# A two-layer decoder trunk: the second layer's attention by heads instead of by groups, its numerators weighted row by row

## The chip, the cores and the metric

The kernel runs on one core of one Trainium2 chip. The metric is the time of an execution on the device, in microseconds (us); lower is better. Before the change three runs took 2020.91, 2022.48 and 2024.51 us. Five engines work side by side, each through a list of instructions of its own: TensorE (PE, matrix products), VectorE (DVE), ScalarE (ACT), GpSimd (POOL) and SyncE (SP, which issues the transfers).

## What is computed

The reference runs two layers over a stream of 1024 positions of 1024 features, in fp32. Layer A is an mLSTM mixer; the change touches it in one place only. Layer B is attention in three dilation groups with eight heads of 128, each followed by a residual and a layer norm. Cut to what matters:

```python
def dilated_block_attention(qb, kb, vb, dilation, n_back, slopes):
    ...
    m = sc.max(-1)
    e = jnp.exp(sc - m[..., None])
    den = e.sum(-1)
    o = jnp.einsum('nbhqk,nbkhd->nbqhd', e, vb.astype(jnp.float32)) / jnp.moveaxis(den, 2, 3)[..., None]
    lse = jnp.moveaxis(m + jnp.log(den), 2, 3)
    return o, lse

def dilated_attention_layer(x, w_in, w_out, kv_blocks, slopes):
    proj = x @ w_in
    q_all = proj[..., :N_GROUPS_B * INNER_B].reshape(bsz, s, N_GROUPS_B, HEADS_B, HEAD_DIM_B)
    z = proj[..., N_GROUPS_B * INNER_B:]
    for g, (window, dilation) in enumerate(GROUPS_B):
        ...
    wts = jax.nn.softmax(jnp.stack(lses), axis=0)
    o = jnp.sum(wts[..., None] * jnp.stack(outs), axis=0).reshape(bsz, s, INNER_B)
    y = o.astype(x.dtype) * jax.nn.silu(z)
    return y @ w_out
```

For every head there are three groups, and in each a softmax over 256 (group 0 and 1) or 128 keys (group 2). The groups' outputs are then mixed by a softmax over their log-sum-exp, row by row; this is the same as dividing the sum of the weighted numerators by the sum of the weighted denominators.

## The kernel before

**Products.** Every large product is made in three passes of reduced precision: an operand is split into a high part (a cast on ScalarE, L93) and a low part (a subtract on VectorE, L94), and `mm3` (L96 to L100) issues high x high, high x low and low x high. On top stands Strassen's scheme with seven products instead of eight: `strassen_steps` (L188) for products of 512 columns, a generator that gives way after each of its seven products (12 matmuls each), and `strassen_wide` (L291) for those of 1024, with 48 matmuls per product, whose weight sums (L313, by `sums`) and result sums (L317) run on VectorE.

**Order.** The program is written once, and a scheduler of the framework then sets the order of each engine's list by a model of its own; `issue_after(x)` keeps what is inside behind instruction x. A tile's slot or a PSUM bank that is given twice makes the second user wait for the first. So the order of the text, the slots and these marks set the order of the work.

**Layer B.** It begins at about 985 us. Two quads of four heads each are the outer loop; inside it come the three groups, and inside a group the four heads. `values(g, quad)` makes the group's values with `strassen_wide` in the first quad, and loads them from memory in the second. Then per head:

- `queries_keys` (a `strassen_steps` of 84 matmuls of 512 columns), with L1201 and L1210 evacuating;
- `scores`: matmuls of 128 columns, row maxima with the bias added (L1260, VectorE), and exponentials with the row sum (L1264, ScalarE) into `stat`;
- `attend`: the blocks of exponentials are transposed on PE (L1278), split, and multiplied by the values (mm3 and the whole matmuls L1301 and L1332); the group's output is copied from PSUM into slot 13 (L1340) and stored to memory as `og`, 512 KB.

After a head's third group, `factors` (L1345) transposes `stat` (L1347), stores it (L1351) and loads it back with eight small transfers. `merge` makes the three groups' factors on 8 partitions and stores them as `f` (L1394). `fetch` loads the three outputs and, spread over 128 partitions, the three rows of factors (512 KB each), and `combine` (L1415 to L1419) multiplies and adds them on VectorE in whole tiles of 128 x 1024, with the gate z last. `by_group` does so for the fourth head. The result, `y2`, is stored.

The gates z are four `strassen_steps` of two heads each. Three of them lie among the groups (`gate_at`); the last, for heads 6 and 7, comes behind all heads, and head 7's attend is interleaved with it. Then follows the output projection: for eight blocks of rows, eight blocks of features `c` and two halves `dm`, `block` issues three matmuls, with operands split by `self.split` in 128 x 1024. Its results are taken up by the layer norm (`begin`, `finish`).

## Time and profile before

| | |
|---|---|
| median of the three runs | 2022.48 us |
| the profiled execution | 2017.29 us |
| its span | 2015.5 us |
| granted clock of PE, mean | 0.996 |
| bytes moved | 300.65 MB |
| layer A, layer B, output projection begin at about | 0, 985, 1915 us |

The profile is of one execution. A row of the timeline has the start, the duration, the engine, the line, the operation and, in brackets, how long the engine had nothing to do before it and what released it. Matmuls overlap, so the duration of one (0.39 us at 512 columns) is longer than the distance to the next. Lines are those of the kernel before, where nothing else is said.

### The profile page before, as it was taken

How to read it: one execution, taken by the hardware profiler on the slowest of the kernel's cores; microseconds unless marked ns; L12 is line 12 of the kernel's file. 1: busy time of each engine (PE TensorE's matmuls, PEld its weight loads, DVE VectorE, ACT ScalarE, POOL GpSimd, SP SyncE). 2: the span in 40 equal slices, each digit the busy share in tenths (PEclk: the TensorE clock that was granted, in tenths of full speed). 3: DMA queues.
4: the chain of work that ended last, by engine and by line, in shares of the span. 5: the costliest groups of instructions: out<-in, count | busy, mean ns of one | idle time of the engine just before them, and what ended most of it. 6: DMA issues, size and time to landing. Idle time of an engine off the chain costs nothing.

```text
span 2015.5 us, 26595 instructions
## 1 busy us (share of the span) xinstructions
PE 1962.4 (97%) x9521; PEld 1626.3 (81%) x9521; DVE 1444.8 (72%) x2854; ACT 992.5 (49%) x1990; POOL 158.7 (8%) x127
## 2 busy tenths in 40 slices
PE   9999999999999999999999999999999999999997
PEld 7778888778888888878788888877887788887776
DVE  8778778675577776457867765776568887776878
ACT  5455555535645543343524542565255456676621
POOL 0200000022145343000000000000000000000000
PEclk9999999999999999999999999999999999999999
DMA  4445464456754543526121143225325622224753
GB/s 170 146 164 193 164 224 172 147 172 227 271 204 164 192 163 117 184 62 232 53 73 53 55 154 106 71 97 178 134 91 203 225 95 85 84 95 154 269 198 126
DMA packets 117916, 300.65 MB, mean 149 GB/s; under 512 B 13652, under 2 KB 31508, under 8 KB 117784
## 3 DMA queue, kind: packets, MB, share of 16 engines
q1 hardware_dynamic: 117784, 298.95, 43.2%
q8 instruction: 75, 1.23, 0.3%
q14 instruction: 57, 0.47, 0.1%
HBM read 206.32 MB, written 92.59 MB: 148 GB/s over the span
## 4 chain that ended last, share of the span: by engine, by line
PE 73%; DVE 12%; DMA 8%; ACT 4%; issue 2%; SPq 0%; POOL 0%; DVEq 0%; ACTq 0%
PE b L98 23%; PE b L100 22%; PE b L99 22%; DVE s L94 3%; DMA s<-in_w_qk 2%; PE b L603 1%; DMA s<-df 1%; ACT s L93 1%; PE b L1278 1%; DMA s<-in_w_z 1%; ACT s L1264 1%; DMA s<-in_xq 1%; PE b L609 1%; PE b L878 1%; DVE s L1415 1%
## 5 line engine op out<-in xcount | busy, mean ns | idle before, releaser
L99 PE MATMUL b<-s,s 128*128 128x512 f32 (+3 forms) x2720 | 1035.3, 382 | 9.2 <-DVE s L94 9.2
L100 PE MATMUL b<-s,s 128*128 128x512 f32 (+3 forms) x2720 | 1021.3, 382 | 4.8 <-DVE s L94 4.7
L98 PE MATMUL b<-s,s 128*128 128x512 f32 (+2 forms) x2720 | 1001.2, 386 | 20.1 <-ACT s L93 16.3
L94 DVE TENSOR_TENSOR s<-s,s 128x512 fp32r<-128x512 f32 (+2 forms) x704 | 507.5, 736 | 279.1 <-ACT s L93 273.4
L93 ACT CAST s<-s 128x512 fp32r<-128x512 f32 (+2 forms) x708 | 436.6, 636 | 541.2 <-PE b L100 308.8
L98 PEld LDWEIGHTS b<-s,s 128*128 128x128 f32 x2720 | 511.7, 188 | 124.7 <-ACT s L93 24.4
L99 PEld LDWEIGHTS b<-s,s 128*128 128x128 f32 x2720 | 512.4, 188 | 107.3 <-DVE s L94 13.2
L100 PEld LDWEIGHTS b<-s,s 128*128 128x128 f32 x2720 | 510.5, 188 | 105.5 <-DVE s L94 9.5
L233 DVE TENSOR_TENSOR s<-s,b 128x512 f32<-128x512 f32 x132 | 89.8, 681 | 27.3 <-PE b L100 25.9
L1264 ACT ACTIVATE s<-s,nmax 128x128 f32<-128x128 f32 (+1 forms) x192 | 84.3, 441 | 45.9 <-DVE nmax L1262 45.6
L94 DVE TENSOR_TENSOR s<-b,s 128x512 fp32r<-128x512 f32 (+1 forms) x96 | 51.5, 552 | 34.7 <-ACT s L93 34.3
L568 DVE SCALAR_TENSOR_TENSOR s<-s,c_convw,s 128x512 f32<-128x512 f32 (+3 forms) x96 | 71.5, 755 | 3.1 <-ACT s L565 2.6
L227 DVE TENSOR_TENSOR s<-s,b 128x512 f32<-128x512 f32 x88 | 59.5, 679 | 16.2 <-PE b L100 11.5
L317 DVE TENSOR_TENSOR s<-s,b 128x512 f32<-128x512 f32 x100 | 63.3, 680 | 8.1 <-PE b L100 7.8
L246 DVE TENSOR_TENSOR s<-s,s 128x512 f32<-128x512 f32 x44 | 30.3, 690 | 50.5 <-DMA s<-in_w_qk 23.5
L812 ACT ACTIVATE s<-s,k 128x128 f32<-128x128 f32 x144 | 47.2, 392 | 39.0 <-DVE s L94 18.5
L313 DVE TENSOR_TENSOR s<-s,s 128x1024 f32<-128x1024 f32 x40 | 49.6, 1247 | 20.8 <-DMA s<-in_w_o 11.7
L1260 DVE CUSTOM_DVE_ANT_0 s<-b,k 128x128 f32<-128x128 f32 (+1 forms) x192 | 57.2, 345 | 6.5 <-PE b L100 4.4
L93 ACT CAST s<-b 128x512 fp32r<-128x512 f32 (+1 forms) x96 | 43.8, 479 | 23.4 <-PE b L100 13.4
L771 POOL TENSOR_TENSOR s<-s 128x512 fp32r<-128x512 f32 x32 | 43.5, 1372 | 75.2 <-ACT s L770 65.5
L1211 DVE SCALAR_TENSOR_TENSOR s<-s,s 128x512 fp32r<-128x512 f32 x48 | 42.4, 885 | 9.6 <-ACT s L1210 9.1
L882 POOL TENSOR_TENSOR s<-s,s 128x512 f32<-128x512 f32 x32 | 42.3, 1337 | 65.0 <-DVE s L881 48.5
(182 smaller groups left out, 1489.0 us busy)
## 6 DMA issues: line engine op xcount, KB each, us to landing
s<-in_w_qk SPq DMA_DIRECT2D x48, 512.0 KB
s<-in_w_out SPq DMA_DIRECT2D x40, 512.0 KB
dp<-s SPq DMA_DIRECT2D x32, 512.0 KB
s<-dp SPq DMA_DIRECT2D x32, 512.0 KB
s<-in_w_v SPq DMA_DIRECT2D x24, 512.0 KB
dg<-s SPq DMA_DIRECT2D x24, 512.0 KB
s<-dg SPq DMA_DIRECT2D x24, 512.0 KB
s<-df SPq DMA_DIRECT2D x24, 512.0 KB
```

What stands on the lines that cost most here:

```text
L93: self.nc.scalar.copy(h, src)
L94: self.last_split = (l_eng or self.nc.vector).tensor_tensor(l, src, f(h), op=ALU.subtract)
L98: mm(ps, lh, rh, start=start, stop=False, skip_group_check=skip)
L99: mm(ps, lh, rl, start=False, stop=False, skip_group_check=skip)
L100: mm(ps, ll, rh, start=False, stop=stop, skip_group_check=skip)
L227: V.tensor_tensor(o, p, q, op=add)
L233: V.tensor_tensor(o, p[lane][rows], q[lane][rows], op=add)
L313: eng.tensor_tensor(o[j], p[j], q[j], op=op)
L317: V.tensor_tensor(o, p, q, op=add)
L568: V.scalar_tensor_tensor(u[i][:, lo:o + 512], xm[i][:, lo - s:o + 512 - s], convw[:, c, 3 - s:4 - s], u[i][:, lo:o + 512], op0=ALU.mult, o ...
L1260: V.tensor_tensor_reduce(out=dst, in0=sc, in1=bias, op0=ALU.add, op1=ALU.max, scale=1.0, scalar=-3e38, accum_out=mx[:, b:b + 1])
L1264: self.last_exp = A.activation(res[b][0], res[b][0], AF.Exp, bias=nm[:, b:b + 1], accum_out=stat[:, 1, g, b:b + 1])
```

## The change

Layer B is written by heads. All three groups' values are made first and stored to memory; then come, for each head, its three groups. A head's attend is delayed by a head: attend to group 0 stands after the products of the next head's first group (or of a gate), to groups 1 and 2 behind the next head's first and second scores.

Since all three groups' row maxima and sums are known by then, the head's factors are made first: `factors` is now a generator in four steps, run beside the next products (behind the third, fourth and sixth of seven). It keeps group 0's rows in place, takes the rows of groups 1 and 2 into that order by a transpose, a store, six small loads and two transposes back, makes the factors on 128 partitions, and takes those of groups 1 and 2 back in the same way. They end as columns, one per block. `attend` then scales each block of exponentials by its column on ScalarE, eight blocks per group, before it transposes them. So a group's outputs only need to be added: group 0 is copied to `acc`, groups 1 and 2 are added from PSUM by VectorE. `og`, the broadcast of `f`, `merge`, `fetch`, `combine`, `by_group` and `weigh` are gone. The values of a head are loaded by `load_values`, four transfers.

At the end, head 7's factors run beside the output projection's blocks for positions 0 and 1, then its attends follow, then the other blocks. The operands' splits of the projection are kept behind the last exponential. The last gates (heads 6 and 7) are now made before head 6's first group.

In layer A, `strassen_wide` gets a mark `late`, set for the second half of the output-gate product: its second product's splits come before two of the weight sums.

Slots and banks are given anew. The core of the diff:

```diff
-        mm(ps, ll, rh, start=False, stop=stop, skip_group_check=skip)
+        self.last_mm = mm(ps, ll, rh, start=False, stop=stop, skip_group_check=skip)
...
-        sums(b12, b22, b12, sub)
-        sums(b11, b12, b11, add)
-        product(a, b21, x["12"], False)
+        if late:
+            product(a, b21, x["12"], False)
+        with self.tc.issue_after(self.last_split.ins) if late else ExitStack():
+            sums(b12, b22, b12, sub)
+            sums(b11, b12, b11, add)
+        if not late:
+            product(a, b21, x["12"], False)
...
+        def load_values(h):
+            cs = slice(h % 4 * P, h % 4 * P + P)
+            res = []
+            for g in range(3):
+                t = self.slot(vs[g], (P, 8, P))
+                rows = self.dram["vn", g, h // 4][:, cs]
...
+                res.append(t)
+            return res
...
-            with self.tc.issue_after(self.last_exp.ins) if first else ExitStack():
-                for half in range(2):
-                    for j in range(2):
-                        ts = slice(2 * j, 2 * j + 2)
-                        self.split(h[:, half, ts], l[:, half, ts], v[half][j][:, :, cs])
+            h, l = [self.slot(s, (P, 8, P), F32R) for s in vhl]
+            for half in range(2):
+                ts = slice(4 * half, 4 * half + 4)
+                self.split(h[:, ts], l[:, ts], t[:, ts])
...
-        def attend(h, g, sp, v):
+        def attend(g, sp, v, factor, acc):
+            for b in range(8):
+                A.activation(sp[b], sp[b], AF.Copy, scale=factor[:, b:b + 1])
...
-            o = self.slot(13)
             for bank in range(2):
                 if g == 0:
-                    A.copy(o[:, 512 * bank:512 * bank + 512], po[bank])
+                    A.copy(acc[:, 512 * bank:512 * bank + 512], po[bank])
                 else:
                     r = 4 if g == 1 else 8
-                    A.copy(o.rearrange("p (i r) -> p r i", r=r)[:, r // 2 * bank:r // 2 * bank + r // 2],
-                           po[bank].rearrange("p (r i) -> p r i", r=r // 2))
-            nc.sync.dma_start(self.dram["og", h, g], o)
...
+            behind = lambda: self.tc.issue_after(self.last_mm.ins)
             pt = self.bank(pS)
+            T.transpose(pt[0:32, 0:P], stat[:, 1:3].rearrange("p g a b -> p (g a b)"), self.ident)
+            V.tensor_copy(rows, pt[0:32, 0:P])
             nc.sync.dma_start(self.dram["st", h], rows)
+            ds = self.dram["st", h].rearrange("(g a b) i -> g a b i", g=2, a=2)
             for kind in range(2):
+                src = ds[0, kind].rearrange("(r hf) (bb i) -> hf bb r i", hf=2, bb=4)
                 for hf in range(2):
+                    o = 8 * kind + 4 * hf
+                    nc.sync.dma_start(r[o:o + 4, 0:128].rearrange("b (r i) -> b r i", r=4), src[hf])
+                self.last_load = nc.sync.dma_start(r[8 * kind:8 * kind + 8, 128:256].rearrange("b (r i) -> b r i", r=8),
+                                                   ds[1, kind].rearrange("r (b i) -> b r i", i=16))
+            yield
+            pt = self.bank(pS)
+            for g in range(2):
+                gs = slice(128 * g, 128 * g + 128)
+                V.tensor_copy(plain(rn[:, gs], g), natural(r[:, gs], g))
+                with behind():
+                    T.transpose(pt[:, 16 * g:16 * g + 16], rn[:, gs], self.ident[0:16, 0:16])
+            sums = pt[:, 0:32].rearrange("p (g a b) -> p g a b", g=2, a=2)
+            V.tensor_tensor(m, stat[:, 0, 0], sums[:, 0, 0], op=ALU.max)
...
+            A.activation(e, e, AF.Exp)
...
+            V.tensor_tensor(e, e, tmp.unsqueeze(1).to_broadcast([P, 3, 8]), op=ALU.mult)
+            yield
+            pt = self.bank(pS)
+            for g in range(2):
+                gs = slice(128 * g, 128 * g + 128)
+                with behind():
+                    T.transpose(pt[0:8, gs], e[:, 1 + g], self.ident)
+                V.tensor_copy(natural(fw[:, gs], g), plain(pt[0:8, gs], g))
+                nc.sync.dma_start(self.dram["f", h][g], fw[:, gs])
...
+            yield
+            pt = self.bank(pS)
+            with behind():
+                T.transpose(pt[:, 0:16], fr, self.ident[0:16, 0:16])
+            V.tensor_copy(fac[:, 1:3], pt[:, 0:16].rearrange("p (g b) -> p g b", g=2))
+            yield [e[:, 0], fac[:, 1], fac[:, 2]]
...
+        class Head:
+            def __init__(self, h, stat, ps):
+                self.h, self.ps = h, ps
+                self.steps = factors(h, stat)
+                next(self.steps)
+            def beside(self, products):
+                for n, _ in enumerate(products):
+                    if n in (2, 3, 5):
+                        self.factors = next(self.steps)
+            def attend(self, g):
+                if g == 0:
+                    self.acc = slot(13)
+                    self.v = load_values(self.h) if self.h == 0 else loaded.pop()
+                attend(g, self.ps[g], head_values(g, self.v[g]), self.factors[g], self.acc)
+                if g < 2:
+                    return
+                z = slot(vs[0])
+                nc.sync.dma_start(z, dram["z2", self.h])
+                V.tensor_tensor(self.acc, self.acc, z, op=ALU.mult)
+                if self.h < 7:
+                    nc.sync.dma_start(dram["y2", self.h], self.acc)
+                    loaded.append(load_values(self.h + 1))
+        slot, dram, loaded = self.slot, self.dram, []
+        for g in range(3):
+            values(g)
...
+        last = None
+        for h in range(HB):
+            stat = self.t(cp, [P, 3, 2, 8], tag="stat", bufs=2)
+            ps = []
             for g in range(3):
+                if last and h in (2, 4, 6) and g == 0:
+                    last.beside(gates(h // 2))
+                    last.attend(0)
+                qk, products = queries_keys(h, g)
+                if last and h not in (2, 4, 6) and g == 0:
+                    last.beside(products)
+                    last.attend(0)
+                for n, _ in enumerate(products):
+                    if (h, g) == (0, 0) and n in (1, 4):
+                        residual(6 + n // 3)
+                ps.append(scores(h, g, qk, stat))
+                if last and g < 2:
+                    last.attend(g + 1)
+            last = Head(h, stat, ps)
...
+            with self.tc.issue_after(self.last_exp.ins):
+                self.split(wh, wl, raw)
+                if c < 7:
+                    self.split(yh, yl, f(yl))
...
-        pss = [[self.bank(2 * i + dm) for dm in range(2)] for i in range(4)]
-        for cs, tbs in ((range(6), (0, 1)), (range(6), (2, 3)), ((6, 7), range(4))):
+        pss = {}
+        def blocks(cs, tbs):
+            for i in tbs:
+                if i not in pss:
+                    pss[i] = [self.bank(2 * i + dm) for dm in range(2)]
             for c in cs:
+                if c == len(yw):
+                    operands(c)
                 for i in tbs:
                     for dm in range(2):
                         block(pss[i][dm], i, dm, c)
+                yield
+        last.beside(blocks(range(7), (0, 1)))
+        for g in range(3):
+            last.attend(g)
+        for cs, tbs in ((range(7), (2, 3)), ((7,), range(4))):
+            for _ in blocks(cs, tbs):
+                pass
```

Three places in the engines' lists. The first is VectorE in layer A's output-gate product: L94 are splits, L313 (L314 after the change) weight sums, L317 (L318) result sums, and the names in brackets are the queues and engines that a row waits for. Before:

```order
L94 TENSOR_TENSOR s_645_3643<-s_586_3188,s_645_3643 128x512 [waits Activation_49]
L94 TENSOR_TENSOR s_648_3670<-s_589_3195,s_648_3670 128x512 [waits Activation_49]
L313 TENSOR_TENSOR s_661_3774<-s_663_3778,s_661_3774 128x1024 [waits DMAHW6_49,DMAHW3_49,DVE_49]
L94 TENSOR_TENSOR s_649_3685<-s_589_3195,s_649_3685 128x512 [waits Activation_49]
L317 TENSOR_TENSOR s_646_3658<-s_591_3199,b_624_3450 128x512 [waits DMAHW2_49,PE_49]
L94 TENSOR_TENSOR s_650_3700<-s_590_3196,s_650_3700 128x512 [waits Activation_49]
```

After:

```order
L94 TENSOR_TENSOR s_660_3870<-s_634_3745,s_660_3870 128x512 [waits DVE_49,Activation_49]
L94 TENSOR_TENSOR s_661_3885<-s_635_3746,s_661_3885 128x512 [waits DMAHW7_49,DVE_49,Activation_49]
L94 TENSOR_TENSOR s_662_3900<-s_635_3746,s_662_3900 128x512 [waits PE_49,Activation_49]
L314 TENSOR_TENSOR s_636_3749<-s_638_3753,s_636_3749 128x1024
L314 TENSOR_TENSOR s_637_3750<-s_639_3754,s_637_3750 128x1024 [waits DMAHW3_49]
L314 TENSOR_TENSOR s_632_3741<-s_636_3749,s_632_3741 128x1024 [waits DVE_49]
L314 TENSOR_TENSOR s_633_3742<-s_637_3750,s_633_3742 128x1024 [waits DVE_49]
L314 TENSOR_TENSOR s_634_3745<-s_634_3745,s_632_3741 128x1024 [waits DVE_49]
L94 TENSOR_TENSOR s_669_3931<-s_632_3741,s_669_3931 128x512 [waits Activation_49]
```

The sum that waits for a load stood among the splits of the product that was being made; now the sums stand behind the last of its splits, one behind the other.

The second place is PE at head 7's last attends: before, L1278 are transposes, L1332 weighted sums, and L98 to L100 with 512 columns are products of the last gates.

```order
L1278 MATMUL b_2713_16435<-c_ident_266,s_2704_16384 128x128 x4
L1347 MATMUL b_2708_16419<-c_ident_266,stat_13317 48x128
L98 MATMUL b_2723_16485<-s_1528_8775,s_2729_16556 128x512
L99 MATMUL b_2723_16485<-s_1529_8776,s_2729_16556 128x512
L1278 MATMUL b_2714_16445<-c_ident_266,s_2704_16384 128x128 x4
L98 MATMUL b_2722_16484<-s_1536_8843,s_2730_16574 128x512
L99 MATMUL b_2722_16484<-s_1537_8844,s_2730_16574 128x512
L1332 MATMUL b_2710_16432<-s_2712_16434,s_2576_15533 128x128 x2
L1332 MATMUL b_2710_16432<-s_2712_16434,s_2577_15534 128x128 x2
L100 MATMUL b_2723_16485<-s_1528_8775,s_2729_16556 128x512
```

After, L1270 are transposes, L1384 and L1395 transposes of the factors, and L98 to L100 with 256 columns are the attend's own products; the row ahead of them is the last of the output projection's blocks for positions 0 and 1.

```order
L100 MATMUL b_2669_16494<-s_2704_16664,s_2707_16667 128x512
L1384 MATMUL b_2691_16604<-c_ident_242,fe_16475 8x128 x2
L1270 MATMUL b_2713_16703<-c_ident_242,s_2580_15965 128x128 x4
L98 MATMUL b_2711_16701<-s_2714_16708,s_2709_16687 128x256
L99 MATMUL b_2711_16701<-s_2714_16708,s_2709_16687 128x256
L100 MATMUL b_2711_16701<-s_2714_16708,s_2710_16688 128x256
L98 MATMUL b_2711_16701<-s_2714_16708,s_2709_16687 128x256
L99 MATMUL b_2711_16701<-s_2714_16708,s_2709_16687 128x256
L100 MATMUL b_2711_16701<-s_2714_16708,s_2710_16688 128x256
L1270 MATMUL b_2718_16732<-c_ident_242,s_2581_15966 128x128 x4
L1395 MATMUL b_2702_16660<-c_ident_242,s_2660_16474 128x16
```

Before, other products stood between the pieces of the attend; now nothing else does until the attends are over.

The third place is ScalarE behind head 7's last exponentials. Before (L1264 are exponentials, L1381 that of `merge`, L1282 and L1340 copies of the attend, L93 casts, L1464 the gate):

```order
L1264 ACTIVATE s_2704_16384,stat_13317<-s_2704_16384,nmax_16385 128x128 x4
L1381 ACTIVATE s_2674_16178<-s_2674_16178 8x384
L1264 ACTIVATE s_2704_16384,stat_13317<-s_2704_16384,nmax_16385 128x128 x4
L93 CAST s_2731_16592<-s_2719_16480 128x512
L93 CAST s_2729_16556<-s_2718_16478 128x512
L93 CAST s_2730_16574<-s_2719_16480 128x512
L1282 COPY s_2712_16434<-b_2713_16435 128x512
L93 CAST s_2739_16636<-s_2738_16635 128x1024
L1282 COPY s_2712_16434<-b_2714_16445 128x512
L1464 ACTIVATE s_2716_16476<-b_2720_16482 128x512
L1340 COPY s_2715_16455<-b_2710_16432 128x4x128
```

After, the last exponentials are followed by the casts of the output projection's operands, of which these are the last, by the exponential of the factors (L1371), and by the scalings (L1260):

```order
L93 CAST s_2700_16640<-s_2701_16641 128x1024
L93 CAST s_2704_16664<-s_2703_16663 128x1024
L93 CAST s_2706_16666<-s_2707_16667 128x1024
L93 CAST s_2750_16956<-s_2749_16955 128x1024
L1371 ACTIVATE fe_16475<-fe_16475 128x24
L1260 ACTIVATE s_2580_15965<-s_2580_15965,fe_16475 128x128
L1260 ACTIVATE s_2580_15965<-s_2580_15965,fe_16475 128x256 x3
L1260 ACTIVATE s_2581_15966<-s_2581_15966,fe_16475 128x256 x4
L93 CAST s_2714_16708<-b_2713_16703 128x512
```

Fourteen casts of 128 x 1024 and two of 128 x 512 now stand between the last exponentials and that of the factors.

278 lines of the change are left out of this document (74 added, 204 removed).

## The prediction

> **What bounds the kernel now.** I read the busy shares first, then what TensorE (PE) waited for, then the windows of 50 us, then single waits in the timeline.
>
> ```profile
> PE 1962.4 (97%) x9521; PEld 1626.3 (81%) x9521; DVE 1444.8 (72%) x2854; ACT 992.5 (49%) x1990; POOL 158.7 (8%) x127
> PE 73%; DVE 12%; DMA 8%; ACT 4%; issue 2%; SPq 0%; POOL 0%; DVEq 0%; ACTq 0%
> ```
>
> PE is busy for 97% of the span and carries 73% of the chain that ended last. The change takes no product out of it, so all that can be won is PE's 53.1 us without work (2015.5 - 1962.4). What released PE when it had waited:
>
> ```profile
> PE b L98 <- ACT s L93: 16.3, 17, 3.1
> PE b L99 <- DVE s L94: 9.2, 8, 2.6
> PE b L100 <- DVE s L94: 4.7, 6, 1.7
> PE b L98 <- DVE s L233: 3.1, 3, 1.7
> ```
>
> Columns: us in total, times, longest. Nearly all of it is the hi/lo split of an operand (L93 on ScalarE, L94 on VectorE) that is late. Where that happens, the windows show (us, PE busy with its count, PEld, DVE, ACT, POOL, granted clock, DMA share, GB/s):
>
> ```profile
> 400.00:450.00 50.00, 47.39 (x204) 38.69 (x203) 37.76 (x52) 16.50 (x28) 13.05 (x7) 0.97 0.49 154
> 1250.00:1300.00 50.00, 49.38 (x239) 41.36 (x238) 37.31 (x73) 24.45 (x51) 0.00 (x0) 1.00 0.29 100
> 1300.00:1350.00 50.00, 47.88 (x253) 40.48 (x251) 37.70 (x95) 33.53 (x82) 0.00 (x0) 1.00 0.28 95
> 1350.00:1400.00 50.00, 47.88 (x241) 39.24 (x240) 34.76 (x71) 27.29 (x64) 0.00 (x0) 1.00 0.48 169
> 1500.00:1550.00 50.00, 48.55 (x252) 40.29 (x251) 39.88 (x101) 28.68 (x64) 0.00 (x0) 1.00 0.55 192
> 1550.00:1600.00 50.00, 46.20 (x218) 37.59 (x217) 45.67 (x99) 23.51 (x48) 0.00 (x0) 0.97 0.67 234
> 1750.00:1800.00 50.00, 48.91 (x268) 41.80 (x267) 38.51 (x104) 37.02 (x92) 0.00 (x0) 1.00 0.18 57
> 1850.00:1900.00 50.00, 44.01 (x225) 35.30 (x224) 41.85 (x100) 26.63 (x52) 0.00 (x0) 1.00 0.70 226
> 1900.00:1950.00 50.00, 49.27 (x230) 40.82 (x229) 40.64 (x62) 23.69 (x38) 0.00 (x0) 1.00 0.78 293
> ```
>
> In the attention (1250 to 1850) these windows lack 0.6 + 2.1 + 2.1 + 1.5 + 3.8 + 1.1 = 11.2 us of PE. 1850 to 1950 lacks 6.7.
>
> **The change part by part.** The sum is made against the profiled execution, 2017.29 us (span 2015.5 and 1.8 around it); it lies 5.2 us below the median of the runs, 2022.48, so I add 5.2 at the end.
>
> *The late sums in layer A.* The one stall of layer A that the edit meets:
>
> ```profile
> 442.08 0.39 PE L100 MATMUL b<-s,s 128*128 128x512 f32 x1
> 442.31 0.39 PE L98 MATMUL b<-s,s 128*128 128x512 f32 x1
> 445.31 0.80 PE L99 MATMUL b<-s,s 128*128 128x512 f32 x1 [2.61 <-DVE s L94]
> ```
>
> ```profile
> 437.54 0.69 DVE L94 TENSOR_TENSOR s<-s,s 128x512 fp32r<-128x512 f32 x1 [0.60 <-ACT s L93]
> 443.42 1.23 DVE L313 TENSOR_TENSOR s<-s,s 128x1024 f32<-128x1024 f32 x1 [5.19 <-DMA s<-in_w_o]
> ```
>
> PE needs a subtract (L94) that is queued on VectorE behind a weight sum (L313), which waits 5.19 us for its load. After the change the subtracts of the product stand ahead of the sums, so the stall goes. A matmul of 512 columns costs 0.23 us, start to start (442.08 to 442.31); the stall is 3.00 - 0.23 = 2.77. Behind it the granted clock was 0.97 over the 50 us, another 1.5 us. Term: -4.3. What is late next are the sums themselves, five in a row at 1.23, ahead of the next product's subtracts; the rest of a product, some 30 matmuls or 7 us, lies over their 6.2, so a part may come back: between -4.3 and -1.
>
> *Small transposes.* The new factor path adds five transposes per head (six for one), 40 in all.
>
> ```profile
> 1570.60 0.27 PE L1347 MATMUL b<-c_ident,stat 128*48 128x128 f32 x1
> 1570.63 0.47 PE L99 MATMUL b<-s,s 128*128 128x512 f32 x1
> 1572.10 1.05 PE L1332 MATMUL b<-s,s 128*128 128x128 f32 x8
> 1572.91 0.48 PE L100 MATMUL b<-s,s 128*128 128x512 f32 x1
> ```
>
> The transpose of the old path held its successor up by 0.03 us, eight small matmuls by 0.81, 0.10 each: 40 cost 1.2 to 4. Term: +2.7.
>
> *The loads and stores of whole tiles.* og (24 stores, 24 loads), 24 broadcasts of f, all 512 KB, go; four loads of a head's values come instead of four larger ones per group and four heads. None of the waits of PE above names a DMA, SP's queue gets shorter, and the values' loads are issued when the head before has ended, some 20 us of products ahead of their use. Term: 0, up to 2 per head if they land late.
>
> *The combination on VectorE goes, scalings on ScalarE come.* This is the largest stall of the attention; VectorE at that time:
>
> ```profile
> 1578.04 1.05 PE L1332 MATMUL b<-s,s 128*128 128x128 f32 x8
> 1581.71 0.80 PE L98 MATMUL b<-s,s 128*128 128x512 f32 x1 [2.62 <-ACT s L93]
> ```
>
> ```profile
> 1576.39 2.35 DVE L1415 TENSOR_TENSOR s<-s,s 128x1024 f32<-128x1024 f32 x2
> 1578.66 1.22 DVE L1417 TENSOR_TENSOR s<-s,s 128x1024 f32<-128x1024 f32 x1
> ```
>
> 3.4 us of combining stand ahead of the evacuation that feeds the cast. Such bursts vanish. In their place come adds from PSUM, 32 of 512 columns in all, and on ScalarE 192 scalings. The trace has no such scaling; the nearest rows are the exponentials of the same tiles and layer A's scaling by a column:
>
> ```profile
> L1264 ACT ACTIVATE s<-s,nmax 128x256 f32<-128x256 f32 x88 | 43.7, 497 | 4.7 <-DVE nmax L1262 4.7
> L1264 ACT ACTIVATE s<-s,nmax 128x128 f32<-128x128 f32 x104 | 40.8, 393 | 41.2 <-DVE nmax L1262 40.9
> L812 ACT ACTIVATE s<-s,k 128x128 f32<-128x128 f32 x144 | 47.2, 392 | 39.0 <-DVE s L94 18.5 <-POOL s L820 10.6 <-DVE mv L851 3.0
> L1340 ACT COPY s<-b 128x512 f32<-128x512 f32 x32 | 35.8, 1120 | 9.7 <-PE b L1301 7.0 <-PE b L1332 2.6
> ```
>
> So 43.7 + 40.8 = 84.5 us come to ScalarE and 35.8 of copies (L1340) leave it: +48.7, or 6 us per head. On average that is nothing: 1750 to 1800, its fullest window of those quoted, had 37.02 of 50. It decides only where a head's scores and the previous head's attention stand close together. For heads 1, 3, 5 and 7 the new order leaves one group's products beside them: 84 matmuls at 0.23, 19 us. The transposes, scores and weighted sums, some 50 small matmuls of 0.10 per group, are 15 more: 34 us. ScalarE at the rate of its fullest window would have 34 x 0.74 = 25 there, and 10.6 (84.5 / 8) - 4.5 (35.8 / 8) more: 31, and some 35 since a whole head's 24 exponentials now stand in one such stretch. Every attend starts with eight scalings in a row, 8 x 0.44 = 3.5 us, before its first transposes. From 0 (perfect overlap) to 8 us (the scalings of each of the last two groups uncovered) per such head; I take 5, above the middle since it is ScalarE's L93 that PE waited longest for; four times 20. Heads 2, 4 and 6 have the gates' products besides: 1 each. After: 23. Before: 11.2, and 1.5 for the clock of 0.97 at 1550: 12.7. Term: +10.3, between -8 and +22.
>
> *The factors' path.* Two trips through memory per head, as before, but now an attend waits for the second instead of a combination behind it. The store of the statistics and the first dependent load:
>
> ```profile
> 1546.76 0.33 SPq L1351 DMA_DIRECT2D ds<-s  x1
> 1549.29 0.29 SPq L1355 DMA_DIRECT2D s<-ds  x1
> ```
>
> 2.5 us from issue to issue, and as much again until the data is there; twice 5 us, beside three to eight steps of products at 2.7 us (12 matmuls each). Hidden in heads 0 to 6. Term: 0; if it is not covered, it shows in the rival C.
>
> *The end.* Before, the last gates' products lie between the pieces of the last attends. After, they are gone to an earlier place, and behind head 7's scores PE has only blocks of the output projection, whose splits are ordered behind the last exponential.
>
> ```profile
> 1870.41 0.40 ACT L1264 ACTIVATE s<-s,nmax 128x128 f32<-128x128 f32 x1 [1.00 <-DVE nmax L1262]
> 1873.12 0.39 ACT L1264 ACTIVATE s<-s,nmax 128x128 f32<-128x128 f32 x1
> 1873.51 0.60 ACT L93 CAST s<-s 128x512 fp32r<-128x512 f32 x1
> ```
>
> ```profile
> L93 ACT CAST s<-s 128x1024 fp32r<-128x1024 f32 x72 | 75.1, 1051 | 49.7 <-DMA s<-in_w_out 35.8 <-DVE s L144 6.4 <-DVE s L94 4.6
> ```
>
> First wait: eight exponentials take 3.1 us, two casts 2.1, and a maximum and hand-overs about 1: 6.3 with PE idle. It is longer than the 2.77 of above, behind which the clock fell: +1.5. The next operand's split (two casts, two subtracts) is about as long as a block step, 1 us of lag. Then ScalarE holds 14 casts of 1.05, 15 us, ahead of the Exp of the factors (L1371), then 24 scalings (10.6 by durations, 8 back to back) and 20 casts and copies of head 7's attend, 9 us at 0.45 (the one of 512 columns above took 0.60): 32 to 35 us with a memory trip of 5 partly beside it. PE has in that time 19 us of blocks (84 x 0.23) and about 10 of attend, with no product between its pieces since the banks 4 to 7 are the attend's. That leaves 3 to 15 idle, with the trip and the hand-overs between pieces; I take 9, and 1.5 for the clock. After: 6.3 + 1.5 + 1 + 9 + 1.5 = 19.3. Before: the 6.7 of 1850 to 1950, and this one:
>
> ```profile
> 1951.66 0.39 PE L100 MATMUL b<-s,s 128*128 128x512 f32 x1
> 1955.19 0.50 PE L98 MATMUL b<-s,s 128*128 128x512 f32 x1 [3.14 <-ACT s L93]
> ```
>
> 9.8 in all. Term: +9.5, between 0 and +20.
>
> The Trainium skill (TensorE: Matmul & The Clock Gate, Part 1: The HAM clock gate) has the clock fall only after an idle window of some 3.4 us that runs free. By that rule a wait of 2.77 should not have halved it, and the trace shows 0.97 behind two waits of under 3 us, so the measurement decides here; by the rule the two clock terms of the end are likely but not certain, and without them the sum is 3 us less.
>
> Sum: 2017.3 - 4.3 + 2.7 + 10.3 + 9.5 = 2035.5; with the 5.2 to the median, **2040.7**.
>
> **The rivals.**
> A, the bursts on VectorE were what hurt, and ScalarE's new work hides. For it: L94, L233 and the combination share VectorE in the quoted stalls, and ScalarE is at half load. Against it: PE waited longest for L93. Then the four clusters cost 1 each (after: 7, term -5.7) and the end costs what it did: 2022.5 - 4.3 + 2.7 - 5.7 + 0 = 2015.
> B, the two sides meet: clusters at 2.5 each (13, term 0) and the end +2: 2022.5 - 4.3 + 2.7 + 2 = 2023.
> C, slower by more: each attend of an odd head waits for its eight scalings and the second trip through memory ends after the products beside it (5 us more on the way to attend 1), so that clusters cost 10 each, 43 with the even heads (term +30), at the end 9.5: 2022.5 - 4.3 + 2.7 + 30 + 9.5 = 2060. It decides from the point where ScalarE's work between two score blocks is longer than PE's.
>
> **How the numbers follow.** Forecast 0.5, A 0.22, B 0.13, C 0.15. A measurement of this kernel tells about 0.2%, 4 us, from no change: faster is A (0.22), same is B (0.13), slower is the forecast and C (0.65). With every term at its end the sum would lie between 2013 and 2066; the range goes down to 2012, 3 under A, and up to C's 2060, and leaves out about 2 in 10.
>
> **What would show it.** In the changed profile: no wait near 442; in the windows of heads 1, 3, 5 and 7 PE below 48 of 50 with waits for L93 casts of transposed tiles or for L1260; behind the last scores a wait of about 6 us; in head 7's attend several waits of 1 to 2 us; PEclk below 1 in the last 100 us. Wrong it would be if PE's idle time in the attention fell under 10 us, or if the last attends ran without waits because ScalarE had the casts done early.

## The result, and the profile after

The changed kernel takes 2082.51 us (four runs, 2081.0 to 2083.93) against 2021.7 of the kernel before: 1.0301 times as long, interval 1.0286 to 1.0315, so 61 us slower. The forecast was 2040.7, in a range that ended at 2060.

The profiled execution has a span of 2080.2 us. The page's busy times:

```profile
PE 2001.3 (96%) x9561; PEld 1647.7 (79%) x9561; DVE 1415.9 (68%) x2815; ACT 1021.8 (49%) x2117; POOL 159.1 (8%) x127
```

VectorE did 29 us less than before and ScalarE 29 more; neither is full. PE's time without work grew from 53 to 79 us, and its own busy time by 39. The mean granted clock fell from 0.996 to 0.987, and a matmul takes longer at a lower clock: behind the wait that ends at 1218.85 those of 512 columns took 0.63 us instead of 0.39. The missing share of the clock times the span is 27 us, against 8 before, so by this estimate the clock makes 19 of the 39. The 40 small transposes can be only a few us; the rest of the 39 I have not traced. What released PE when it had waited (us in total, times, longest):

```profile
PE b L98 <- ACT s L93: 23.7, 33, 3.7
PE b L98 <- DVE s L233: 9.7, 7, 3.3
PE b L99 <- DVE s L94: 8.3, 13, 1.4
PE b L1348 <- ACT s L1254: 5.5, 1, 5.5
PE b L98 <- DVE s L227: 3.2, 1, 3.2
```

The first row had 17 waits before and has 33 now: beside one of 3.7, all are under 1.5 us, most between 0.4 and 1.1. The windows of 50 us show where (PE is the second number, the granted clock the third from the end):

```profile
400.00:450.00 50.00, 50.00 (x222) 41.44 (x221) 38.14 (x53) 18.05 (x30) 13.05 (x7) 1.00 0.54 182
1200.00:1250.00 50.00, 46.12 (x194) 36.71 (x193) 38.19 (x55) 15.28 (x27) 0.00 (x0) 0.97 0.53 179
1300.00:1350.00 50.00, 47.34 (x231) 38.15 (x230) 28.98 (x66) 27.33 (x74) 0.00 (x0) 1.00 0.13 41
1350.00:1400.00 50.00, 45.32 (x242) 37.76 (x241) 38.38 (x98) 31.21 (x79) 0.00 (x0) 1.00 0.33 106
1500.00:1550.00 50.00, 45.51 (x232) 36.19 (x232) 32.09 (x79) 31.88 (x79) 0.00 (x0) 1.00 0.14 44
1700.00:1750.00 50.00, 43.50 (x236) 35.49 (x235) 29.88 (x80) 31.94 (x84) 0.00 (x0) 1.00 0.18 55
1900.00:1950.00 50.00, 41.17 (x236) 34.49 (x234) 29.90 (x93) 32.26 (x88) 0.00 (x0) 0.96 0.49 162
1950.00:2000.00 50.00, 39.70 (x165) 31.77 (x166) 27.80 (x45) 33.70 (x73) 0.00 (x0) 0.76 0.35 124
```

Layer A's stall is gone (47.39 at a clock of 0.97 before, 50.00 at 1.00 now). Every odd head's stretch (1300 to 1400 is head 1, 1500 head 3, 1700 head 5, 1900 head 7) lacks 4 to 9 us of PE, and so does the end; 1200, where the gates' first products run, is new. The even heads' stretches lose less, but not nothing (1450 lacks 2.9 and 1800 lacks 4.3). In none of the windows shown is ScalarE more than 34 of 50 busy. The cause is to be read from the factors' path of one head, which begins behind head 0's last exponentials. These are its rows on VectorE (the copies of the transposed statistics, of the loaded rows, the arithmetic, the copies of the transposed factors, and the factors' column):

```profile
1306.10 0.27 DVE L1349 COPY s<-b 32x128 f32<-32x128 f32 x1
1311.53 0.26 DVE L1363 COPY s<-s 16x128 f32<-16x128 f32 x1 [0.18 <-DMA s<-ds]
1312.18 0.26 DVE L1363 COPY s<-s 16x128 f32<-16x128 f32 x1 [0.39 <-DMA s<-ds]
1316.59 0.16 DVE L1367 TENSOR_TENSOR s<-stat,b 128x8 f32<-128x8 f32 x1 [0.24 <-PE b L1365]
...
1322.14 0.18 DVE L1378 TENSOR_TENSOR fe<-fe,s 128x24 f32<-128x24 f32 x1
1326.90 0.38 DVE L1385 COPY s<-b 8x128 f32<-8x128 f32 x1
1331.66 0.35 DVE L1385 COPY s<-b 8x128 f32<-8x128 f32 x1
1337.19 0.17 DVE L1396 COPY ff<-b 128x16 f32<-128x16 f32 x1 [3.40 <-PE b L1395]
```

From 1306.1 to 1337.4 it takes 31 us; behind heads 1 to 6 it takes 30 to 35. The two trips through memory are 5.4 (1306.10 to 1311.53) and 5.5 (1331.66 to 1337.19). The 20 between them are operations of 0.2 to 0.4 us that wait for a place among the products: 4 to 5 us for each of the transposes ahead of 1316.59, 1326.90 and 1331.66, 5.6 for eleven small operations on VectorE and an exponential on ScalarE. Part of this waiting may be the program's own: from the second step on, the transposes carry the mark `behind`, which keeps them behind the last product's matmul written ahead of them. No run leaves out the marks alone. One group's products are 19 us. On ScalarE this then follows:

```profile
1337.03 0.59 ACT L93 CAST s<-b 128x512 fp32r<-128x512 f32 x1 [4.07 <-PE b L1270]
1337.51 0.60 ACT L1197 ACTIVATE s<-b 128x512 f32<-128x512 f32 x1
1338.00 4.04 ACT L1260 ACTIVATE s<-s,ff 128x128 f32<-128x128 f32 x12
1341.94 0.35 ACT L93 CAST s<-b 128x256 fp32r<-128x256 f32 x1
```

ScalarE idles for 4.07 us and then has twelve scalings in a row ahead of a cast that PE waits for. Two readings offer themselves: the scalings are too much (theory S, the one that the forecast's terms rest on), or the path is too long and presses the attends together (theory L).

### The profile page after: what moved, and what is told of

It is laid out like the page before. It is cut to its first block, busy times and chain, and to the rows that moved or that the text cites. A ratio compares the mean times of both kernels' runs of the same rounds, so it can differ in the third digit from the quotient of the medians.

```text
span 2080.2 us, 26718 instructions
## 1 busy us (share of the span) xinstructions
PE 2001.3 (96%) x9561; PEld 1647.7 (79%) x9561; DVE 1415.9 (68%) x2815; ACT 1021.8 (49%) x2117; POOL 159.1 (8%) x127
## 4 chain that ended last, share of the span: by engine, by line
PE 80%; DVE 9%; ACT 5%; DMA 5%; issue 1%; SPq 0%; DVEq 0%; ACTq 0%
PE b L98 25%; PE b L100 25%; PE b L99 25%; DVE s L94 3%; PE b L606 1%; ACT s L93 1%; ACT s L1260 1%; DMA s<-in_w_qk 1%; PE b L1270 1%; DMA s<-in_w_z 1%; DVE s L1250 1%; PE b L612 1%; PE b L882 1%; PE b L1324 1%; DVE s L1201 1%
## 5 line engine op out<-in xcount | busy, mean ns | idle before, releaser
L98 PE MATMUL b<-s,s 128*128 128x512 f32 (+2 forms) x2720 | 1011.0, 389 | 38.4 <-ACT s L93 23.7
L100 PE MATMUL b<-s,s 128*128 128x512 f32 (+3 forms) x2720 | 1029.3, 384 | 2.9 <-DVE s L94 2.9
L93 ACT CAST s<-s 128x512 fp32r<-128x512 f32 (+3 forms) x675 | 433.3, 658 | 576.3 <-PE b L100 335.0
L94 DVE TENSOR_TENSOR s<-s,s 128x512 fp32r<-128x512 f32 (+4 forms) x671 | 503.9, 765 | 280.4 <-ACT s L93 277.8
L98 PEld LDWEIGHTS b<-s,s 128*128 128x128 f32 x2720 | 515.3, 190 | 150.1 <-ACT s L93 34.1
L100 PEld LDWEIGHTS b<-s,s 128*128 128x128 f32 x2720 | 515.1, 190 | 105.1 <-DVE s L94 7.2
L94 DVE TENSOR_TENSOR s<-b,s 128x512 fp32r<-128x512 f32 (+1 forms) x96 | 52.3, 552 | 46.1 <-ACT s L93 45.9
L227 DVE TENSOR_TENSOR s<-s,b 128x512 f32<-128x512 f32 x88 | 59.8, 682 | 15.9 <-PE b L100 11.3
L318 DVE TENSOR_TENSOR s<-s,b 128x512 f32<-128x512 f32 x100 | 63.2, 680 | 10.2 <-PE b L100 5.6
L93 ACT CAST s<-b 128x512 fp32r<-128x512 f32 (+1 forms) x96 | 44.3, 474 | 40.8 <-PE b L1270 25.9
L314 DVE TENSOR_TENSOR s<-s,s 128x1024 f32<-128x1024 f32 x40 | 49.5, 1249 | 10.2 <-DMA s<-in_w_v 5.8
L1200 ACT ACTIVATE s<-s 128x512 fp32r<-128x512 f32 x48 | 42.4, 884 | 18.4 <-DVE s L233 17.7
L1270 PE MATMUL b<-c_ident,s 128*128 128x128 f32 x280 | 45.8, 285 | 4.1 <-DVE s L1385 1.6
```

The lines of the kernel that those rows point to most:

```text
L93: self.nc.scalar.copy(h, src)
L94: self.last_split = (l_eng or self.nc.vector).tensor_tensor(l, src, f(h), op=ALU.subtract)
L98: mm(ps, lh, rh, start=start, stop=False, skip_group_check=skip)
L100: self.last_mm = mm(ps, ll, rh, start=False, stop=stop, skip_group_check=skip)
L227: V.tensor_tensor(o, p, q, op=add)
L318: V.tensor_tensor(o, p, q, op=add)
```

## The experiments

**The part in layer A alone.** In the kernel before, the edit of `strassen_wide` and its mark, and nothing else.

```diff
+        if late:
+            product(a, b21, x["12"], False)
+        with self.tc.issue_after(self.last_split.ins) if late else ExitStack():
+            sums(b12, b22, b12, sub)
+            sums(b11, b12, b11, add)
```

> The kernel before with only the edit in layer A: the second product of the output-gate stage ahead of its two weight sums. Theory A (the stall at 442 us and the half clock behind it are all that this edit touches, and nothing comes back): 4.3 us under the kernel before, about 2017.4. Rival (the sums, five in a row, now hold up the next product, or the time is lost again in layer B because something else is waited for): within 2 us of the kernel before.

2017.38 us, 0.9983 times the kernel before (0.9973 to 0.9993): 3.4 us faster, about what the stall and its half clock had cost. PE is full from 400 to 500, at a clock of 1.00, so the sums don't come back there. It is the one version here that leaves nothing out and is faster than both kernels.

**The scalings, four ways.** A fixed column in place of the factors:

```diff
-                A.activation(sp[b], sp[b], AF.Copy, scale=factor[:, b:b + 1])
+                A.activation(sp[b], sp[b], AF.Copy, scale=self.ident[:, b:b + 1])
```

> The changed kernel, each block of numerators still scaled on ScalarE, 192 scalings, but by a fixed column instead of the head's factors; the weighting by the factors is so left out, while the factors are still made and carried through memory. It takes away the wait for the factors and leaves ScalarE its work. Theory L (the factors are ready about 31 us behind the last scores, so that three attends crowd into what is left of the head; the crowding is the loss): most of the 43 us that the attention lost goes, about 2045. Theory S (ScalarE's added work, 48.7 us in bursts ahead of the casts that PE needs, is the loss wherever it stands): under 10 us gained, 2073 or more.

No scalings:

```diff
-            for b in range(8):
-                A.activation(sp[b], sp[b], AF.Copy, scale=factor[:, b:b + 1])
```

> The changed kernel without the 192 scalings at all; the weighting by the factors is left out, while the factors are still made. It takes away both the wait for the factors and ScalarE's work. Theory L: as with the fixed column, at most 5 us less. Theory S: 40 us under the changed kernel, about 2042, and 30 or more under the one with the fixed column. If both parts matter, it lies under the fixed column by 5 to 20 us.

On GpSimd:

```diff
-                A.activation(sp[b], sp[b], AF.Copy, scale=factor[:, b:b + 1])
+                G.tensor_scalar_mul(sp[b], sp[b], factor[:, b:b + 1])
```

> The changed kernel with the 192 scalings on GpSimd, which has nothing else to do in layer B, in place of ScalarE; the result is the same. The wait for the factors stays, ScalarE has 84 us less to do. Theory S: the odd heads' clusters lose 3 to 5 us each instead of 11 to 13, in all 20 to 35 us under the changed kernel, 2048 to 2062. Theory L: the attends stay as late as they were, within 8 us of the changed kernel, or slower where one scaling takes GpSimd longer (its rows of 512 columns took 1.37 us, so some 0.4 to 0.6 for 128 to 256).

And added to the kernel before, at the head of its `attend`:

```diff
+            for b in range(8):
+                A.activation(sp[b], sp[b], AF.Copy, scale=self.ident[:, b:b + 1])
```

> The kernel before, whose order of groups spreads one attend and one score block per product, with 192 scalings by a fixed column added on ScalarE ahead of each attend's transposes; its result so has one factor too many. It adds the work of the change without its order. If ScalarE's scalings cost the same wherever they stand: 25 us over the kernel before, 2045. If they cost only where attends crowd and at the uncovered end: under 8 us over it, 2021 to 2028.

Measured: fixed column 2082.96 (1.0309 times before, 1.0291 to 1.0327), no gain; without scalings 2057.96 (1.0193, 1.0175 to 1.0211), on GpSimd 2062.71 (1.0201, 1.0184 to 1.0219), 20 to 25 us faster; added to the kernel before 2017.3 (0.999, 0.9978 to 1.0002), nothing. After the first three theory S seemed right in kind, though the gain was less than the 40 us that it had put down, and L refuted. The fourth contradicts S: the same 192 scalings are free in another order. And the trace of the fixed column showed that it was no clean test. Its PE rows at head 0's first attend (L1384 and L1395 are transposes of the path, L1270 those of the attend):

```profile
1329.55 0.27 PE L1384 MATMUL b<-c_ident,fe 128*8 128x128 f32 x1
1334.91 0.60 PE L1270 MATMUL b<-c_ident,s 128*128 128x128 f32 x4
1335.67 0.23 PE L1395 MATMUL b<-c_ident,s 16*128 16x16 f32 x1
1335.83 0.66 PE L1270 MATMUL b<-c_ident,s 128*128 128x128 f32 x4
```

All of head 0's scalings were done at 1308.3; these are the last eight, group 2's:

```profile
1303.81 0.39 ACT L1260 ACTIVATE s<-s,c_ident 128x128 f32<-128x128 f32 x1
...
1306.15 2.15 ACT L1260 ACTIVATE s<-s,c_ident 128x128 f32<-128x128 f32 x7
```

Yet the attend still began in the midst of the path, 27 us later. `factors` and `attend` take their banks from the same ring of two (`pS`), in the order of the text.

**Without the path.** `Head` makes no factors and `beside` only runs the products; the scalings by a fixed column stay, and then go too.

```diff
-                self.steps = factors(h, stat)
-                next(self.steps)
+                self.factors = [self_ident[:, 8 * g:8 * g + 8] for g in range(3)]
...
-                for n, _ in enumerate(products):
-                    if n in (2, 3, 5):
-                        self.factors = next(self.steps)
+                for _ in products:
+                    pass
```

> The changed kernel without the factors' path (no transposes of the statistics, no trips through memory, none of the small operations) and with the 192 scalings by a fixed column; the weighting by the factors is left out. The fixed-column run still had the factors' transposes, and they share two PSUM banks in turn with the attends' transposes, so the attends stood where they had stood. Here nothing holds an attend back. Theory L (the factors' path holds the attends back and presses them and the next scores into the second half of a head; ScalarE's scalings cost only there): 25 to 40 us under the changed kernel, 2042 to 2057. Theory S (the scalings cost in this order of heads anyway): no more than 10 us less, what the path's own instructions take.

> As the run without the factors' path, and without the scalings too. Theory L: within 8 us of that run, since scalings that are not pressed together hide, as they did in the kernel before. Theory S: 20 us or more under it. Against the kernel before, what is left over is the order by heads alone with its end: the stall at 1215 (6.5) and some 15 to 20 at the end.

2003.11 us with the scalings (0.9909 times before, 0.9889 to 0.9929) and 2002.52 without (0.9907, 0.9887 to 0.9927). That is twice what theory L had put down, and the 192 scalings cost 0.6 us. The windows of the run with the scalings:

```profile
1300.00:1350.00 50.00, 50.00 (x265) 42.84 (x264) 37.15 (x86) 34.11 (x91) 0.00 (x0) 1.00 0.16 53
1350.00:1400.00 50.00, 50.00 (x275) 43.13 (x274) 36.47 (x87) 32.24 (x84) 0.00 (x0) 1.00 0.32 106
1700.00:1750.00 50.00, 50.00 (x261) 42.52 (x260) 36.29 (x79) 31.43 (x78) 0.00 (x0) 1.00 0.34 112
1850.00:1900.00 50.00, 38.86 (x203) 32.77 (x202) 37.34 (x79) 38.97 (x87) 0.00 (x0) 0.86 0.71 263
1900.00:1950.00 50.00, 49.68 (x254) 42.03 (x253) 19.99 (x29) 8.91 (x22) 0.00 (x0) 1.00 0.04 11
```

PE is full through every odd head, with ScalarE busier than in the changed kernel (34.11 and 32.24 of 50 against 27.33 and 31.21). What is left is the end, which lacks 11.1 us at a clock of 0.86, and the window at 1200, which lacks 4.3. With the scalings, the path costs 79 us (2082.51 against 2003.11); without them it costs 55 (2057.96 against 2002.52). So the whole loss hangs on the path, and the scalings cost their 25 us only where the path is: theory S, by which they cost wherever they stand, falls. These runs take away everything that the path is at once: its place ahead of the attends, its banks and its work.

**What of the path.** The trips replaced by copies of wrong rows; the first attend written ahead of the path, with a fixed column; and, with the result kept, the first attend ahead of the path's last step, with both transposes of the third step ahead of their copies.

```diff
-            nc.sync.dma_start(self.dram["st", h], rows)
...
+            V.tensor_copy(r[:, 0:128], rows[0:16])
+            V.tensor_copy(r[:, 128:256], rows[0:16])
...
-                nc.sync.dma_start(self.dram["f", h][g], fw[:, gs])
...
+            V.tensor_copy(fr, rn[:, 0:128])
```

```diff
+                    last.attend(0)
                     last.beside(gates(h // 2))
-                    last.attend(0)
...
+                    last.attend(0)
                     last.beside(products)
-                    last.attend(0)
```

```diff
-                with behind():
-                    T.transpose(pt[0:8, gs], e[:, 1 + g], self.ident)
+                T.transpose(pt[0:8, gs], e[:, 1 + g], self.ident)
+            for g in range(2):
+                gs = slice(128 * g, 128 * g + 128)
...
-                    if n in (2, 3, 5):
+                    if n in (2, 3):
                         self.factors = next(self.steps)
+                    if n == 4:
+                        self.attend(0)
+                        self.factors = next(self.steps)
```

> The changed kernel with the factors' two trips through memory replaced by copies on VectorE that put the wrong rows in the tiles, so the factors of groups 1 and 2 are not the head's; everything else of the path stays. Theory M (the trips, 5 to 6 us each of a path of 32, make the factors late): 15 to 30 us under the changed kernel. Theory B (the path is a chain of six small transposes and some twenty small operations, each of which waits for its place behind products on TensorE and VectorE, and it holds the two banks of the attends' transposes meanwhile; the trips lie beside that): within 6 us.

> The changed kernel with scalings by a fixed column, as in the fixed-column run, but with each head's first attend written ahead of the factors' steps, so that its transposes take the two shared banks before the factors' do. All of the path's instructions are still there; the weighting by the factors is left out. Theory B (the banks, not the data, kept the attends late in the fixed-column run): 25 us or more under that run, 2058 or less. Rival (the path's own instructions on TensorE, VectorE and the queue are what costs): within 10 us of it, 2073 or more.

> The changed kernel with the first attend's transposes ahead of the factors' last step: group 0 needs no trip back, so its attend is written behind the fifth product and before the last transpose of the factors, and both transposes of the third step stand ahead of their copies. The result is the same. Theory L: the first attend starts some 4 to 8 us earlier, 5 to 15 us under the changed kernel. Theory S: within 4 us.

2056.2 without trips (1.0175, 1.0149 to 1.0202), 2050.39 with the attend first (1.0155, 1.0133 to 1.0178), 2060.15 with the first attend early (1.0192, 1.0168 to 1.0215): 26, 33 and 22 us. All three are larger than the rivals allowed, and the last is larger than theory L's 5 to 15, too; it takes the mark `behind` from the third step's transposes as well, and the two were not run apart. The attend-first run has all of the path's instructions, and loses 33 us less than the fixed column that differs from it only in the order of the text: so much the path costs by standing ahead of the first attend. But it is still 47 us over the run without the path (2003.11). In it the path stands ahead of the second and third attends, so whether these 47 are its place there or its work is not shown. Without the trips the path is 21 to 23 us long behind heads 0 to 6; that this gains 26 us refutes the second half of theory B. Making the path shorter helps, and so does taking an attend from behind it; the bank and the place in PE's list were not told apart, since the order of the text sets both.

**Products beside it.** The attends one per group; and the three mends together (first attend early, scalings and rows on GpSimd), with the gates' products in front of heads 0, 2, 4 and 6 or beside heads 1, 3, 5 and 7.

```diff
-                ps.append(scores(h, g, qk, stat))
-                if last and g < 2:
-                    last.attend(g + 1)
+                if last and g:
+                    last.attend(g)
+                ps.append(scores(h, g, qk, stat))
```

```diff
-                if last and h in (2, 4, 6) and g == 0:
-                    last.beside(gates(h // 2))
+                if last and h in (1, 3, 5, 7) and g == 0:
+                    last.beside(gates((h - 1) // 2))
```

> The changed kernel, the attends written one per group: attend to group g behind the products of the next head's group g, where the change has two beside the first group's scores, one beside the second's and none beside the third's. Theory C (two attends and a score block between two products are more than the products beside them cover; the rest of the attention's loss is this crowding): 10 to 20 us under the changed kernel, 2063 to 2073. Rival (the small pieces' hand-overs cost the same wherever they stand): within 4 us.

> The changed kernel with three mends at once: the first attend early, the scalings on GpSimd, the residual rows on GpSimd. The result is the same. If the parts add: 2082 less 22 (scalings), 4 (rows) and 5 to 10 (first attend), 2046 to 2052; still over the kernel before, since the end and the order by heads stay.

> The run with the three mends (first attend early, scalings and residual rows on GpSimd), and the gates' products moved from in front of heads 0, 2, 4 and 6 to heads 1, 3, 5 and 7, which have had only one group's products beside the factors' path. The result is the same. If it is products beside the path that a head lacks: heads 1, 3, 5 and 7 lose 1 to 2 us instead of some 12, heads 2, 4 and 6 the reverse; one more head is covered and the stall at 1215 is gone, so 12 to 20 us under the run with the three mends, 2035 to 2043. If not: within 5 us of it.

One attend per group: 2079.29 (1.0291, 1.0276 to 1.0307), the rival's number; but the scheduler had put the pieces at nearly the same rows, so the run decides nothing. The three mends: 2055.26 (1.0164, 1.0138 to 1.019), 27 us under the changed kernel; they don't add. Gates at the odd heads: 2053.69 (1.0173, 1.0151 to 1.0196), no gain, but the windows moved. With the gates at the even heads:

```profile
1450.00:1500.00 50.00, 50.00 (x254) 42.18 (x252) 37.09 (x89) 25.69 (x63) 0.00 (x0) 1.00 0.28 86
1700.00:1750.00 50.00, 45.26 (x252) 37.50 (x250) 36.12 (x102) 30.81 (x82) 15.03 (x16) 1.00 0.24 74
1800.00:1850.00 50.00, 50.00 (x267) 42.81 (x266) 36.21 (x88) 27.08 (x59) 2.70 (x5) 1.00 0.27 81
```

At the odd heads:

```profile
1450.00:1500.00 50.00, 46.10 (x231) 37.17 (x230) 35.77 (x90) 26.61 (x64) 8.48 (x8) 1.00 0.30 97
1700.00:1750.00 50.00, 50.00 (x265) 42.82 (x264) 36.52 (x86) 28.33 (x68) 0.86 (x2) 1.00 0.28 85
1800.00:1850.00 50.00, 45.06 (x225) 36.42 (x226) 35.12 (x97) 23.58 (x62) 2.16 (x3) 1.00 0.31 101
```

With two groups' products (38 us) beside the path PE is full; with one (19 us) it is not, whichever of heads 1 to 6 that is. Counted from the beginning of one path to that of the next, PE lacks 4.8 to 5.5 us in each such stretch with one group and at most 1.0 with two. The path, 29 to 33 us long beside one group, lies between. The stretch of head 7 is an exception: it lacks 8.1 without the gates and 7.5 with them, so the fourth head covered is no gain.

**The end, and the stall at 1215.** The operands' splits without the mark `issue_after(self.last_exp.ins)`; the residual rows on GpSimd.

```diff
-            with self.tc.issue_after(self.last_exp.ins):
-                self.split(wh, wl, raw)
-                if c < 7:
-                    self.split(yh, yl, f(yl))
+            self.split(wh, wl, raw)
+            if c < 7:
+                self.split(yh, yl, f(yl))
```

```diff
-            self.scale_row(r, *gain0)
+            G.tensor_tensor(r, r, gain0[0], op=ALU.mult)
+            G.tensor_tensor(r, r, gain0[1], op=ALU.add)
```

> The changed kernel without the mark that keeps the splits of the output projection's operands behind the last exponential. Theory E (the wait of 5.7 us behind the last scores and 1.9 us more ahead of the first block is the price of that mark): 5 to 8 us under the changed kernel, 2075 to 2077. Rival (the operands' slots, which hold the stream until the last product is done, or ScalarE's list set the moment anyway): within 2 us.

> The changed kernel with the multiply and add of the residual rows (four whole tiles of 128 x 1024 on VectorE between the first gates' products, two more pairs later) on GpSimd. Theory R (the stall of 3.4 us at 1215 and the half clock behind it come from a product's evacuation that stands behind these two operations on VectorE): about 6.5 us under the changed kernel, 2076. Rival (the evacuation is late for another reason, or GpSimd is too slow and the row is waited for): no more than 2 us.

2084.71 without the mark (1.0314, 1.0293 to 1.0335): no gain. The wait of 5.5 for the last exponential gave way to another, of the factors' first transpose for its loads:

```profile
PE b L1365 <- DVE s L1363: 7.8, 2, 7.4
```

So at the end PE waits for the path once the last exponential no longer holds it. The rows on GpSimd: 2078.66 (1.0291, 1.0273 to 1.0309), which cannot be told from the changed kernel's 1.0301; see the last section.

**The path out of the way.** All of the order by heads, with the result kept: groups 1 and 2 take group 0's row maximum as the shift of their exponentials, so that the numerators need no factors. The maximum is known after a head's first scores and goes through memory beside the next products; the row sums' reciprocal is multiplied in at the end.

```diff
-                V.tensor_scalar_mul(nm[:, b0:b0 + n], mx[:, b0:b0 + n], -1.0)
+                if g == 0:
+                    V.tensor_scalar_mul(nm[:, b0:b0 + n], mx[:, b0:b0 + n], -1.0)
...
+                if g == 1:
+                    next(moved)
+                ps.append(scores(h, g, qk, stat, shift))
+                if g == 0:
+                    moved = shifts(h, shift)
+                    next(moved)
...
+                nc.sync.dma_start(fb, dram["n", self.h].to_broadcast([P, SEQ]))
+                V.tensor_tensor(self.acc, self.acc, fb, op=ALU.mult)
...
-        last.beside(blocks(range(7), (0, 1)))
-        for g in range(3):
-            last.attend(g)
+        for n, _ in enumerate(blocks(range(7), (0, 1))):
+            if n == 4:
+                next(last.steps)
+            if n in (0, 2, 4):
+                last.attend(n // 2)
```

So head 7's attends also move: they stand between the output projection's blocks, no longer behind them.

> The order by heads with no factors ahead of the attends: groups 1 and 2 take group 0's row maximum, brought into their order while the next group's products run, as the shift of their exponentials, so all three groups' numerators are on one scale and are added as they are; the row sums go through memory beside later products, and their reciprocal, one row of 1024 spread over the partitions, is multiplied in behind the gate. Softmax does not depend on the shift, so the result is the same. Theory B (what costs is the factors' path between the last scores and the attends): about as fast as the run with neither factors nor scalings, 2002 to 2010, faster than the kernel before by 12 us or more. Rival (the wait only moves: the second and third groups' exponentials wait for the shift, or the last head for its sums): 2020 or more.

The second run of the pair has the rows elsewhere, too:

```diff
-        for n, _ in enumerate(gates(0)):
-            if n in (1, 4):
-                residual(4 + n // 3)
+        for _ in gates(0):
+            pass
```

> As the run with the common shift, and the residual rows' multiply and add moved from between the first gates' products to between the first head's products, where the attention's other small work has not begun. Theory R (the stall at 1215 and the half clock behind it, 6 us in that stage, come from those operations standing ahead of a product's evacuation): 4 to 6 us under the run with the common shift. Rival (they only stall another product): within 2 us of it.

2034.01 (1.0059, 1.0044 to 1.0074) and 2032.26 (1.0048, 1.0032 to 1.0065). It takes back 49 of the 61 us, but stays 12 over the kernel before. So the number is the rival's, but the rival's waits are not seen: the end lacks no more than without the path (5.0 us at a clock of 0.86 from 1900 to 1950), and no wait of ScalarE's exponentials ends with the moved shift. What ended their waits are the row maxima (16.7 us) and group 0's own shift (27.8), together less than the 61.6 for the maxima in the run without the path. What PE waits for is in pieces:

```profile
PE b L98 <- DVE s L233: 10.0, 11, 2.2
PE b L100 <- DVE s L94: 7.4, 8, 1.7
PE b L98 <- ACT s L93: 7.3, 12, 1.3
```

These I have not traced further, so what makes this run 31 us slower than the one without the path stays open; beside its own trips through memory it has one more load and one more multiply of a whole tile per head. The second run does not test theory R: the scheduler put the rows where they had been. Their multiplies begin at 1215.54 and their adds at 1219.02 on VectorE, and PE's wait of 2.57 us for the evacuation behind them is still there, at 1222.12.

## Why the prediction was wrong, point by point

The first reading, that nearly all of PE's waiting is a split that is late, covers 30 of its 53 us (16.3 + 9.2 + 4.7). The direction was right, but that is luck in part, since the largest loss that it set down in the attention was the scalings'. The signs that it named came: waits for L93 in the odd heads' windows, a wait of some 6 us behind the last scores (5.5), a clock below 1 at the end. They are as much the signs of a late path as of too many scalings, and could not tell the two apart.

- *Layer A*, -4.3: right, -3.4 measured (1.4 to 5.5).
- *Small transposes*, +2.7, and *whole tiles' transfers*, 0: not measured apart. In layer B no wait of PE names a transfer.
- *Scalings in the clusters*, +10.3: the mechanism was wrong. The place was right (odd heads, one group's products, waits for L93), and rows that fitted the reading stood in the profile after. But in the same order by heads, with one group's products beside the odd heads, 192 scalings cost 0.6 us without the path, and nothing in the kernel before; the 20 to 25 us that they cost in the changed kernel come only together with the path.
- *The factors' path*, "Hidden in heads 0 to 6. Term: 0": **this is the step that failed.** It was summed as two trips of 5 us against the products beside it. The trips were right (5.4 and 5.5); the 20 us in which its small operations wait for their places were left out, and so was that the attends share its two banks. So the path is 30 to 35 us long, where one group's products are 19. The term is 79 us by the run without the path; 26 of them go with the trips alone, and 22 to 33 by moving the first attend ahead of the path or of its last step. These parts overlap, and what share the banks have stays open. Rival C named the path, at 5 us on the way to one attend, and gave 2060.
- *The end*, 19.3, of which 16.3 are waits and 3 the clock: from 1946 to 2006, behind the last scores, PE lacks 13.7 us, and the clock of 0.80 costs 12 more. So the waits were about right (the first, set down as 6.3, was 5.5), and the clock was set down too low. ScalarE's list was longer than said: fifteen casts of 1024 columns stand ahead of the factors' exponential, not fourteen, and from the last exponential to the last attend's transposes it is 49 us instead of 32 to 35. Only a part of this price is the path's: without it 11.1 are lacking at the end, and 7 by the clock.
- What no term had: the order by heads without the path is 18 us faster than the kernel before. I put this down to the bursts of combining on VectorE, which are gone, and to the products that every head's attends find beside them, but no run shows it apart: 3.4 of the 18 are layer A's, and that run also leaves out work that the kernel before has. And the stall at 1215, 3.9 us in its window and a clock of 0.97: the residual rows had been moved between the first gates' products. On VectorE they wait 2.73 us for the load of the norm's gain, and then stand ahead of the evacuation (L227) that PE waits for:

```profile
1212.27 2.36 DVE L948 TENSOR_TENSOR s<-s,s 128x1024 f32<-128x1024 f32 x2 [2.73 <-DMA s<-in_ln_g]
...
1215.75 2.35 DVE L949 TENSOR_TENSOR s<-s,s 128x1024 f32<-128x1024 f32 x2
1218.02 0.68 DVE L227 TENSOR_TENSOR s<-s,b 128x512 f32<-128x512 f32 x1
```

The Trainium skill's rule on the clock (TensorE: Matmul & The Clock Gate, Part 1: The HAM clock gate), that it falls only after an idle window of some 3.4 us, made the end's clock terms uncertain; they came, and larger, behind waits of 5.5 and 3.7 us, which agrees with it. The wait at 1215 was shorter, 3.20 us, and the clock of its window was 0.97 all the same; there the measurement decides.

## What to carry to other kernels

A path of many small dependent steps can cost the waiting for a place at every one of them, on engines whose lists are full of other work: count its steps by the distance from one of its rows to the next in a busy stretch, not by their durations. Compare that length with the work that can be done beside it, and look at what it holds meanwhile (a bank, a slot). An engine that is in every wait's name need not be the cause: leave its work out, and leave out what makes it late, each alone and both together, before believing it.
